# Small vectors in one load, a routing without POOL's splits, and a first weight chunk split under the last output tile

## The chip, the core and the metric

The kernel runs on one core of a Trainium2 chip. TensorE (PE, with its weight loads as PEld), VectorE (DVE), ScalarE (ACT), GpSimd (POOL) and SyncE (SP, which only issues loads here) work in parallel, each through its own list of instructions in a fixed order. The metric is the device time of one launch in microseconds; lower is better.

## The reference

One layer over 2048 tokens of width 1024: a modulated layer norm, a Hyena mixer (projection, short convolution, two long convolutions with filters that a small sine network makes, output projection), a residual with layer norm, and a mixture of 16 experts in which each expert chooses its 256 tokens. Cut to what the change touches:

```python
a = sin(freq * (z @ f_w1 + f_b1))                 # the filter network, three layers of 64
for n in range(2):
    a = sin(freq * (a @ f_w2[n] + f_b2[n]))
m = split(silu(c) @ mod_w + mod_b, 6)             # shift and scale of the layer norms
hl = layer_norm(x + pos) * (1 + m[1]) + m[0]
u = conv3(hl @ w_in + b_in, conv_w, conv_b)       # ... long convolutions, output projection, norm
aff = softmax(h @ w_router)                       # (2048, 16)
gate, idx = top_k(aff.T, 256)                     # expert choice: 256 tokens for each expert
xe = h[idx]
ye = ((silu(xe @ w1) * (xe @ w3)) @ w2) * gate    # w1, w3: 1024 x 2048, w2: 2048 x 1024, per expert
out = layer_norm(alpha * x + (1 + m[5]) * scatter_add(ye, idx))
```

All is fp32. A product of two fp32 matrices is made of three products of shortened numbers: `h` is the operand cast to fp32r, `l` what is left (operand minus cast), and hh + hl + lh is summed.

## The kernel before

The kernel is one long program for one core. Most of it goes through a scheduler that sets the order on each engine; the routing and the first expert's gathering stand in the order in which they are written (`manual_schedule`).

**Start (0 to about 117 us).** `early_mod` computes the shift and scale of the first norm: 16 loads `mw` of 512 KB (five buffers), of which five are multiplied with `sg` on PE (L462, 8 one-column products each) and eleven on DVE (`macc`, L464 and L467); 16 one-column products (L470) then sum `macc` over the partitions, and L473 adds `mb` and gives `md`. `filter_acts` runs the sine network in four pieces of 512 positions per layer: PE (L209), ACT `turn` (L211), two DVE steps `kk` (L213, L214), ACT sine (L215); its small vectors `fb` are six loads of four-byte elements on ACT's queue (L193 to L195). `side_steps` adds the position embedding to x on POOL (L496, L497), takes the statistics on DVE (L376, L377), makes 1/sqrt in `rstd_steps` (L383 to L392: `lva`, `lsq`, `r`, `nb`), normalises on ACT (L506), transposes on PE (L522) and modulates with `md` on ACT (L526). The projection's biases and convolution weights `prm` (L593 to L595) are loaded on ACT's queue too, and `cs` and `mb` (L445, L448) on SP's.

**Output stage (to about 1772 us).** 16 tiles of 128 tokens; of each tile two norms (`norm1`, `norm2`, L1167 to L1191), transposes (`turn`, L1221 and L1222), router logits (L1230, L1232) and their gathering (L1238, L1239). At n == 16 the generator `moe_start` loads the first expert's first chunk (SP) and makes POOL's constants and `tri`, `ii`, `blkb` (DVE, L1428 to L1430). After the loop, ACT loads the table for Exp (L1270).

**Routing (1772 to about 1847 us).** `phase_route` makes the softmax, packs each affinity into two 16-bit halves `half`, and searches the 256th largest of each expert two bits at a time: 7 rounds on the upper half, 8 on the lower. A round counts on DVE how many values reach each of three candidates (L1320, three instructions), sums the counts over an expert's partitions on PE (`cp`, L1322), compares with 256 (`ge` and `num`, L1338) and makes the next candidates (`base` L1335, `cand` L1342, with `thr` L1328 in the shadow of PE). Meanwhile the weights of chunks 0 and 1 of expert 0 are split: three casts each on ACT (L1400), three subtractions each on POOL (L1401).

**Experts (from about 1847 us).** Each of the 16 experts goes through 8 chunks of 256 hidden columns: SP loads w1, w3, w2 (L1391; two raw buffers for w1 and w3, one for w2), ACT casts and DVE subtracts, PE projects (L1502, L1503) and multiplies back (L175 to L177). `route(0)` comes first: it selects indices (PE, DVE), POOL gathers the 256 rows `xg` (L1472), PE transposes them in four groups through one PSUM buffer `tp` (L1482), and ACT and DVE split each group into `xs` (L1484, L1485).

## Time and profile before

| | us |
|---|---|
| median of 3 runs (lowest, highest) | 4089.68 (4086.54, 4090.18) |
| the profiled execution | 4085.04 |
| its span in the profile | 4083.2 |
| PE busy, whole span | 3833.0 (94%) |
| DVE busy | 2789.9 (68%) |
| ACT busy | 1940.8 (48%) |
| POOL busy | 1040.3 (25%) |
| start, 0 to 117: PE busy | 58.53 |
| middle, 117 to 1660: PE busy of 1543 | 1468.22 |
| output stage's end, 1660 to 1772: PE busy of 112 | 100.76 |
| routing and gathering, 1772 to 1847: PE busy of 75 | 8.03 |

The span runs from the first to the last instruction of the core; the profiled execution's own time has 1.84 us around it. PE is busy nearly all the time but for three places: the start, the routing, and the last 83 us. In those the other engines' order decides. Times in the rows below are microseconds from the start of the span.

### The profile page before, as it was taken

The page shows a single profiled execution, that of the slowest core. Times are in us where ns is not written, and L with a number is a line of the kernel's source. Part 1 is how long each engine was busy: PE and PEld are TensorE (multiplying, and loading weights), DVE is VectorE, ACT ScalarE, POOL GpSimd, SP SyncE. Part 2 cuts the span into 40 slices and gives each one's busy share as a digit, 9 for nine tenths or more (in the row PEclk, how much of TensorE's full clock was granted, in tenths as well). Part 3 has the DMA queues.
Part 4 walks back from the last instruction along what each step waited for, and adds up shares of the span by engine and source line. Part 5 has one row for each costly group of instructions (what it writes and reads, how often), then busy time and mean ns, then how long its engine had stood idle before and what let it go on. Part 6 is the DMA issues. An engine that isn't in the chain of part 4 may idle for free.

```text
span 4083.2 us, 52931 instructions
## 1 busy us (share of the span) xinstructions
PE 3833.0 (94%) x19839; PEld 3171.7 (78%) x19839; DVE 2789.9 (68%) x4017; ACT 1940.8 (48%) x2845; POOL 1040.3 (25%) x1092
## 2 busy tenths in 40 slices
PE   4899999999999989939999999999999999999997
PEld 3666766777777877827888888888888888888896
DVE  5777876776877877785666666666666666656766
ACT  3544543333777651114555555555555555544443
POOL 2355552212455442220000000000000000014635
PEclk8999999999999999969999999999999999999999
DMA  6355656667999986445666665666566656656764
GB/s 201 113 175 173 179 172 210 221 205 227 268 283 278 294 251 203 136 162 167 196 193 209 206 196 188 214 204 195 188 215 203 195 189 213 203 176 221 238 228 159
DMA packets 620796, 831.73 MB, mean 204 GB/s; under 512 B 56627, under 2 KB 506947, under 8 KB 618236
## 3 DMA queue, kind: packets, MB, share of 16 engines
q1 hardware_dynamic: 545594, 661.93, 50.8%
q0 software_dynamic: 57088, 163.48, 13.7%
q10 hardware_dynamic: 17858, 2.95, 0.5%
q8 instruction: 156, 2.56, 0.3%
q14 instruction: 100, 0.82, 0.1%
HBM read 643.82 MB, written 150.75 MB: 195 GB/s over the span
## 4 chain that ended last, share of the span: by engine, by line
PE 75%; DVE 9%; issue 5%; DMA 4%; POOL 3%; ACT 3%; SPq 0%; ACTq 0%; POOLq 0%; DVEq 0%
PE ab L1502 19%; PE ab L1503 10%; PE acc L175 5%; PE acc L176 5%; PE acc L177 5%; PE ip L175 3%; PE ip L177 3%; PE ip L176 3%; PE sp L335 2%; PE xp L854 2%; PE ap L889 2%; PE xp L872 2%; PE op L175 1%; PE op L177 1%; PE op L176 1%
## 5 line engine op out<-in xcount | busy, mean ns | idle before, releaser
L1502 PE MATMUL ab<-xs,w3h 128*128 128x512 f32 x1664 | 600.6, 399 | 0.0
L1502 PE MATMUL ab<-xs,w1h 128*128 128x512 f32 x1664 | 598.2, 399 | 0.0
L1401 DVE TENSOR_TENSOR w2l<-w2r,w2h 128x2048 fp32r<-128x2048 f32 x126 | 297.6, 2362 | 267.0 <-ACT w2h L1400 266.9
L1503 PE MATMUL ab<-xs,w3l 128*128 128x256 f32 x1664 | 468.2, 281 | 0.0
L1503 PE MATMUL ab<-xs,w1l 128*128 128x256 f32 x1664 | 466.6, 280 | 0.0
L175 PE MATMUL acc<-w2h,hh 128*128 128x512 f32 x1024 | 404.1, 395 | 14.3 <-ACT hh L170 13.8
L176 PE MATMUL acc<-w2l,hh 128*128 128x512 f32 x1024 | 402.5, 393 | 0.0
L177 PE MATMUL acc<-w2h,hl 128*128 128x512 f32 x1024 | 399.5, 391 | 0.8 <-DVE hl L171 0.8
L1502 PEld LDWEIGHTS ab<-xs,w3h 128*128 128x128 f32 x1664 | 313.0, 188 | 76.6
L1502 PEld LDWEIGHTS ab<-xs,w1h 128*128 128x128 f32 x1664 | 313.0, 188 | 72.9
L1548 POOL DMA_INDIRECT accd<-y,idx x27 | 68.5, 2535 | 1101.8 <-DVE y L1542 1095.6
L1401 DVE TENSOR_TENSOR w1l<-w1r,w1h 128x2048 fp32r<-128x2048 f32 x126 | 301.0, 2389 | 62.7 <-ACT w1h L1400 62.6
L170 ACT CAST hh<-u 128x256 fp32r<-128x256 f32 x256 | 104.1, 407 | 478.6 <-DVE u L1525 478.6
L1503 PEld LDWEIGHTS ab<-xs,w1l 128*128 128x128 f32 x1664 | 314.2, 189 | 7.1
L1506 DVE TENSOR_TENSOR u<-ab,u 128x256 f32<-128x256 f32 x416 | 174.6, 420 | 205.2 <-ACT u L1505 196.8
L1503 PEld LDWEIGHTS ab<-xs,w3l 128*128 128x128 f32 x1664 | 314.8, 189 | 0.0
L1401 DVE TENSOR_TENSOR w3l<-w3r,w3h 128x2048 fp32r<-128x2048 f32 x126 | 292.9, 2324 | 18.7 <-ACT w3h L1400 18.7
L1400 ACT CAST w2h<-w2r 128x2048 fp32r<-128x2048 f32 x128 | 244.1, 1907 | 94.7 <-PE acc L177 86.3
L1400 ACT CAST w1h<-w1r 128x2048 fp32r<-128x2048 f32 x128 | 244.5, 1910 | 80.5 <-PE ab L1502 79.0
L1400 ACT CAST w3h<-w3r 128x2048 fp32r<-128x2048 f32 x128 | 244.5, 1910 | 68.4 <-PE ab L1502 66.3
L1505 ACT COPY u<-ab 128x256 f32<-128x256 f32 x416 | 152.8, 367 | 184.9 <-PE ab L1503 184.8
L175 PE MATMUL ip<-hh,wh 128*128 128x512 f32 x576 | 237.4, 412 | 3.3 <-ACT hh L170 3.3
(399 smaller groups left out, 9114.7 us busy)
## 6 DMA issues: line engine op xcount, KB each, us to landing
w1r<-in_moe_w_dram SPq DMA_DIRECT2D x128, 1024.0 KB
w3r<-in_moe_w_dram SPq DMA_DIRECT2D x128, 1024.0 KB
w2r<-in_moe_w_dram SPq DMA_DIRECT2D x128, 1024.0 KB
fud<-ev SPq DMA_DIRECT2D x128, 256.0 KB
kr<-fud SPq DMA_DIRECT2D x64, 512.0 KB
bn<-ao POOLq DMA_DIRECT2D x248, 128.0 KB, 7.2
win<-in_c_win_dram SPq DMA_DIRECT2D x64, 256.0 KB
mw<-in_mod_w_dram SPq DMA_DIRECT2D x64, 256.0 KB
```

Source lines behind the costliest of these rows:

```text
L170: nc.scalar.copy(hi, raw)
L175: nc.tensor.matmul(out, lhsT=ah, rhs=bh, start=start, stop=False)
L176: nc.tensor.matmul(out, lhsT=ah, rhs=bl, start=False, stop=False)
L177: nc.tensor.matmul(out, lhsT=al, rhs=bh, start=False, stop=stop)
L335: nc.tensor.matmul(p, lhsT=s1[:, th], rhs=hb[th], start=True, stop=(n0 > 0))
L854: nc.tensor.matmul(p[:, i], lhsT=s2[:, 2 * gp + i], rhs=r[:, i], start=True, stop=True)
L1400: nc.scalar.copy(h, raw)
L1401: eng.tensor_tensor(l, raw, f_(h), OP.subtract)
L1502: nc.tensor.matmul(p, lhsT=ws[2 * j][:, k, fs], rhs=xs[:, k], start=(k == 0), stop=False)
L1503: nc.tensor.matmul(p[:, 0], lhsT=ws[2 * j + 1][:, k, fs], rhs=xs[:, k, 0], start=False, stop=(k == 7))
L1505: nc.scalar.copy(u, p[:, 1])
L1506: nc.vector.tensor_tensor(u, p[:, 0], u, OP.add)
```

## The change

1. **One load for small vectors.** The host lays c, mod_b, conv_w, conv_b, b_in, freq, b1 and b2 side by side in `c_small` (128 x 148), and SP loads it once in place of `cs`, `mb`, the six `fb` and the three `prm` loads.
2. **Small steps.** `kk` is one instruction of another kind (the scaled one with two tensors), and `rstd_steps` takes the square root with the constant as a bias on ACT, straight from `stat`, with fewer DVE steps behind it.
3. **End of the output stage.** Exp's table is loaded at n == 17, and there the casts of the first chunk's w1 and w3 (ACT) and their subtractions (DVE) are written; `tri`, `ii`, `blkb` follow them.
4. **Routing.** POOL's six subtractions are gone. The third count of a round is made on ACT (Sign with a sum), the other two on DVE count what lies below the candidate; PE sums them with two products; `ge` compares with a small tile `lim`; the third candidate's constants are 0.5 lower.
5. **Expert 0.** `route(0, wide=True)` puts groups 1 to 3 of the transposes into the three buffers `ab`; the cast of chunk 0's w2 stands on ACT behind the signs, its subtraction and those of chunk 1's w1 and w3 on DVE behind the splits of `xs`; chunk 1's w2 is split when chunk 1 is taken. On SP the load of chunk 2's w1 stands ahead of that of chunk 1's w2.

ACT's list at the start, before (the rows from the silu of c on; `fb`, `prm` are the small vectors, `fw`, `zt` the filter network's weights and input):

```order
L446 ACTIVATE sg<-cs 128x8
L193 DMA fb<-in_hy_f_freq_dram 64x1
L194 DMA fb<-in_hy_f_b_dram 64x1
L195 DMA fb<-in_hy_f_b_dram 64x2x1
...
L211 ACTIVATE turn<-sp,frq 128x512
L593 DMA prm<-in_hy_conv_w_dram 128x72x1
L594 DMA prm<-in_hy_conv_b_dram 128x24x1
L595 DMA prm<-in_hy_b_in_dram 128x24x1
L215 ACTIVATE a_459<-kk 128x512 x2
```

and now:

```order
L445 ACTIVATE sg<-small 128x8
L200 DMA zt<-in_c_z_dram 66x1024
L203 DMA fw_116<-in_hy_f_w_dram 64x64
L205 DMA fw_117<-in_hy_f_w_dram 64x64 x2
L203 DMA fw_116<-in_hy_f_w_dram 64x64
L205 DMA fw_118<-in_hy_f_w_dram 64x64 x2
L215 ACTIVATE turn<-sp,frq 128x512
L215 ACTIVATE turn<-g,frq 128x512
L215 ACTIVATE turn<-sp,frq 128x512
L219 ACTIVATE a_446<-kk 128x512
```

Nine issues of small loads have left ACT's list, three of them from between the first turns and the first sine.

PE's list at the start, before, from the fourth `mw` product's neighbours to the transposes of x (`a` and `zt` hold the first and second layer's results):

```order
L209 MATMUL sp<-a_459,fw_119 128x512
L209 MATMUL g<-a_459,fw_119 128x512
L462 MATMUL sd<-sg,mw 128x1 x8
L209 MATMUL sp<-a_459,fw_119 128x512
L209 MATMUL g<-a_459,fw_119 128x512
L470 MATMUL sd<-ones_f,macc_170 128x1 x8
L470 MATMUL sd<-ones_f,macc_171 128x1 x8
L209 MATMUL sp<-zt,fw_120 128x512
L209 MATMUL sp<-zt,fw_121 128x512
L522 MATMUL sd<-ident,x 128x128 x16
```

and now, the same stretch:

```order
L459 MATMUL sd<-sg,mw 128x1 x8
L213 MATMUL sp<-zt,fw_117 128x512
L213 MATMUL sp<-zt,fw_118 128x512
L213 MATMUL g<-zt,fw_117 128x512
L213 MATMUL g<-zt,fw_118 128x512
L213 MATMUL sp<-zt,fw_117 128x512
L213 MATMUL sp<-zt,fw_118 128x512
L467 MATMUL sd<-ones_f,macc_163 128x1 x8
L467 MATMUL sd<-ones_f,macc_164 128x1 x8
L519 MATMUL sd<-ident,x 128x128 x32
```

Six products of the network's third layer now stand ahead of the sums over the partitions, where before two stood behind them.

ACT's list at the end of the output stage, before (`ht` and `lp`, `lg` belong to the last tile's transposes and logits):

```order
L1179 ACTIVATE r<-r 128x1
L1239 COPY lg<-rp 128x32
L1222 COPY ht<-tp 128x4x128 x2
L1232 COPY lp<-rp 128x256
L1239 COPY lg<-rp 128x32
L1270 ACT_TABLE_LOAD
L1270 ACTIVATE r<-ident 128x1
L1287 ACTIVATE lg<-lg 128x256
L1400 CAST w1h<-w1r 128x2048
L1400 CAST w3h<-w3r 128x2048
L1400 CAST w2h<-w2r 128x2048
```

and now:

```order
L1175 ACTIVATE r<-r 128x1
L1256 ACT_TABLE_LOAD
L1256 ACTIVATE r<-ident 128x1
L1437 CAST w1h<-w1r 128x2048
L1437 CAST w3h<-w3r 128x2048
L1235 COPY lg<-rp 128x32
L1218 COPY ht<-tp 128x4x128 x2
L1228 COPY lp<-rp 128x256
L1235 COPY lg<-rp 128x32
L1285 ACTIVATE lg<-lg 128x256
L1318 ACTIVATE sign,cs<-half_15054,kc 128x256
L1318 ACTIVATE sign,cs<-half_15054,cand 128x256 x6
```

The table load and two casts have moved ahead of the last tile's copies, and signs stand where the casts of both chunks stood.

The diff, cut to its core:

```diff
@@ -166,6 +166,16 @@
+def host_small(x):
...
+    col = lambda v: np.asarray(v, dtype=np.float32).reshape(-1, 128).T
+    two = lambda v: np.concatenate([np.asarray(v, dtype=np.float32).reshape(-1, 64).T] * 2, 0)
+    return np.ascontiguousarray(np.concatenate(
+        [col(x["c"][0]), col(x["mod_b"][0, 0:2048]), col(x["hy_conv_w"][0]), col(x["hy_conv_b"][0]), col(x["hy_b_in"][0]),
+         two(x["hy_f_freq"][0]), two(x["hy_f_b1"][0]), two(x["hy_f_b2"][0])], 1))
@@ -177,10 +187,9 @@
+def filter_acts(tc, A, fb, ld, ps, afw, arv):
-    fb = ld.tile([128, 4], F32, name="fb")
@@ -188,11 +197,6 @@
-    for s in range(2):
-        sl = slice(s * 64, s * 64 + 64)
-        nc.scalar.dma_start(fb[sl, 0:1], A["hy_f_freq"][0].unsqueeze(1))
-        nc.scalar.dma_start(fb[sl, 1:2], A["hy_f_b1"][0].unsqueeze(1))
-        nc.scalar.dma_start(fb[sl, 2:4], A["hy_f_b2"][0].rearrange("i k -> k i"))
@@ -211,7 +215,7 @@
-        nc.vector.tensor_tensor(kk, turn, kk, OP.subtract)
+        nc.vector.scalar_tensor_tensor(kk, kk, -1.0, turn, op0=OP.mult, op1=OP.add)
@@ -379,16 +383,13 @@
-    va = wk.tile([128, n], F32, name="lva")
-    nc.vector.tensor_scalar(va, stat[:, :, 1], eps, None, op0=OP.add)
+    nc.scalar.activation(r, stat[:, :, 1], AF.Sqrt, bias=eps)
+    yield 1
...
-    nc.scalar.activation(sq, va, AF.Sqrt)
-    yield 1
-    nc.vector.reciprocal(r, sq)
-    nc.vector.tensor_tensor(sq, r, r, OP.mult)
-    nc.vector.tensor_tensor(sq, sq, va, OP.mult)
-    nc.vector.tensor_scalar(sq, sq, -0.5, 1.5, op0=OP.mult, op1=OP.add)
-    nc.vector.tensor_tensor(r, r, sq, OP.mult)
+    nc.vector.reciprocal(r, r)
+    nc.vector.scalar_tensor_tensor(sq, stat[:, :, 1], eps, r, op0=OP.add, op1=OP.mult)
+    nc.vector.scalar_tensor_tensor(sq, sq, -0.5, r, op0=OP.mult, op1=OP.mult)
+    nc.vector.scalar_tensor_tensor(r, sq, 1.5, r, op0=OP.add, op1=OP.mult)
@@ -589,10 +588,7 @@
-        prm = S.top.tile([128, 5, 24], F32, name="prm")
-        nc.scalar.dma_start(prm[:, 0:3], A["hy_conv_w"][0].rearrange("j (k p) -> p j k", p=128))
-        nc.scalar.dma_start(prm[:, 3], A["hy_conv_b"][0].rearrange("(k p) -> p k", p=128))
-        nc.scalar.dma_start(prm[:, 4], A["hy_b_in"][0].rearrange("(k p) -> p k", p=128))
+        prm = S.small[:, 24:144].rearrange("p (j k) -> p j k", j=5)
@@ -1256,7 +1252,8 @@
-            if n == 16:
+            if n == 17:
+                nc.scalar.activation(wk.tile([128, 1], F32, name="r"), ident[:, 0:1], AF.Exp)
@@ -1266,8 +1263,6 @@
-        sq = wk.tile([128, 1], F32, name="r")
-        nc.scalar.activation(sq, ident[:, 0:1], AF.Exp)
@@ -1281,11 +1276,13 @@
+        lim = wk.tile([128, 3], F32, name="lim")
+        nc.gpsimd.memset(lim[:, 0:2], T - CAP + 0.5)
+        nc.gpsimd.memset(lim[:, 2:3], T - 2.0 * CAP + 1.0)
...
-        next(R.split_first)
@@ -1314,12 +1311,17 @@
-                cnt = wk.tile([128, 3], BF16, name="cnt", bufs=2)
-                for k in range(3):
+                cnt = wk.tile([128, 2], BF16, name="cnt", bufs=2)
+                cs = wk.tile([128, 1], BF16, name="cs", bufs=2)
+                sign = wk.tile([128, 256], BF16, name="sign")
+                with nc.allow_low_precision(reason="whole numbers of at most 256"):
+                    nc.scalar.activation(sign, v, AF.Sign, scale=-1.0, bias=cand[:, 2:3], accum_out=cs)
+                for k in range(2):
...
-                    nc.vector.tensor_scalar(junk, v, cand[:, k:k + 1], 0.0, op0=OP.is_ge, op1=OP.add, accum_out=cnt[:, k:k + 1])
+                    nc.vector.tensor_scalar(junk, v, cand[:, k:k + 1], 0.0, op0=OP.is_lt, op1=OP.add, accum_out=cnt[:, k:k + 1])
...
-                nc.tensor.matmul(p, lhsT=blkb, rhs=cnt, start=True, stop=True)
+                nc.tensor.matmul(p[:, 2:3], lhsT=blkb, rhs=cs, start=True, stop=True)
+                nc.tensor.matmul(p[:, 0:2], lhsT=blkb, rhs=cnt, start=True, stop=True)
@@ -1335,7 +1337,7 @@
-                nc.vector.tensor_scalar(ge, p, CAP - 0.5, 0.0, op0=OP.is_ge, op1=OP.add, accum_out=num)
+                nc.vector.scalar_tensor_tensor(ge, p, 1.0, lim, op0=OP.mult, op1=OP.is_le, accum_out=num)
@@ -1422,18 +1424,30 @@
-            nc.gpsimd.memset(R.kc[:, n, k:k + 1], float((k + 1) << (14 - 2 * n)))
+            nc.gpsimd.memset(R.kc[:, n, k:k + 1], float((k + 1) << (14 - 2 * n)) - 0.5 * (k == 2))
...
+    hs = [(n, raw, wt.tile(list(raw.shape), F32R, name=n + "h"), wt.tile(list(raw.shape), F32R, name=n + "l")) for n, raw in raws]
...
+    def sub(i):
+        _, raw, h, l = hs[i]
+        nc.vector.scalar_tensor_tensor(l, raw, 1.0, f_(h), op0=OP.mult, op1=OP.subtract)
...
+    for i in range(2):
+        nc.scalar.copy(hs[i][2], hs[i][1])
+    for i in range(2):
+        sub(i)
...
+    R.first = [t for h in hs for t in h[2:]]
...
-    R.first = []
-    for n in range(2):
-        R.first.append(split(raws, nc.gpsimd))
-        if n == 0:
-            raws = load(0, 1)
+    nc.scalar.copy(hs[2][2], hs[2][1])
+    yield
+    sub(2)
+    raws = load(0, 1)
+    R.second = split(raws[:2])
+    R.raw = raws[2:]
@@ -1441,14 +1455,15 @@
-        with tc.manual_schedule():
-            phase_route(tc, ident, ones_f, lg, R)
+        order = st.enter_context(ExitStack())
+        order.enter_context(tc.manual_schedule())
+        phase_route(tc, ident, ones_f, lg, R)
@@ -1475,7 +1490,7 @@
-                p = ps.tile([128, 2, 256], F32, name="tp", bufs=1)
+                p = ps.tile([128, 2, 256], F32, name="ab", bufs=3) if wide and q else ps.tile([128, 2, 256], F32, name="tp", bufs=1)
@@ -1586,9 +1601,14 @@
-        with tc.manual_schedule():
-            for _ in route(0):
-                pass
+        first = route(0, wide=True)
+        next(first)
+        next(R.split_first)
+        next(first)
+        for _ in first:
+            pass
+        next(R.split_first)
+        order.close()
@@ -1603,7 +1623,10 @@
-                ws = R.first.pop(0) if R.first else R.split(R.load(e, fc))
+                if e == 0 and fc < 2:
+                    ws = (R.second + R.split(R.raw)) if fc else R.first
+                else:
+                    ws = R.split(R.load(e, fc))
@@ -1740,6 +1763,8 @@
+            S.small = S.top.tile([128, 148], F32, name="small")
+            nc.sync.dma_start(S.small, A["c_small"])
```

## Rows read from the trace of the kernel before

**Rows 1.** Windows: us, busy of PE, PEld, DVE, ACT, POOL, clock, DMA, GB/s

```profile
1772.00:1847.00 75.00, 8.03 (x35) 5.60 (x36) 60.01 (x206) 13.47 (x11) 28.96 (x8) 0.51 0.50 168
1847.00:4000.00 2153.00, 2139.80 (x11961) 1853.33 (x11961) 1365.86 (x1665) 1079.22 (x1364) 267.66 (x226) 1.00 0.63 202
```

**Rows 2.** Timeline, ACT, start: start, us, instruction, idle before, releaser

```profile
24.28 0.78 ACT L211 ACTIVATE turn<-sp,frq 128x512 f32<-128x512 f32 x1 [19.03 <-DMA fw<-in_hy_f_w_dram]
...
25.60 15.20 ACTq L594 DMA_DIRECT2D prm<-in_hy_conv_b_dram  x1
...
43.01 1.15 ACT L215 ACTIVATE a<-kk 128x512 f32<-128x512 f32 x2 [16.61 <-issue]
```

**Rows 3.** Timeline, PE, start of the kernel

```profile
12.41 3.55 PE L462 MATMUL sd<-sg,mw 128*128 128x1 f32 x16 [10.54 <-DMA mw<-in_mod_w_dram]
15.81 2.06 PE L209 MATMUL sp<-zt,fw 66*128 66x512 f32 x2
...
47.07 1.84 PE L462 MATMUL sd<-sg,mw 128*128 128x1 f32 x16
...
56.78 6.99 PE L470 MATMUL sd<-ones_f,macc 128*128 128x1 f32 x32 [6.04 <-DVE macc L467]
77.30 3.78 PE L209 MATMUL sp<-zt,fw 128*128 128x512 f32 x4 [13.53 <-ACT zt L215]
```

**Rows 4.** Timeline, DVE, start of the kernel

```profile
63.80 0.24 DVE L473 SCALAR_TENSOR_TENSOR md<-sd,mb 128x8 f32<-128x8 f32 x2 [4.62 <-PE sd L470]
...
67.02 8.04 DVE L383 TENSOR_SCALAR lva<-stat 128x4 f32<-128x4 f32 x1
...
80.31 0.15 DVE L392 SCALAR_TENSOR_TENSOR nb<-stat,r 128x4 f32<-128x4 f32 x1
```

**Rows 5.** Timeline, POOL, start: the first of six such additions in a row

```profile
67.69 1.27 POOL L496 TENSOR_TENSOR x<-x,pr 128x512 f32<-128x512 f32 x1
```

**Rows 6.** Timeline, ACT, end of the output stage and start of the routing

```profile
1767.94 0.58 ACT L1222 COPY ht<-tp 128x512 f32<-128x512 f32 x1 [4.07 <-PE tp L1221]
...
1772.03 1.28 ACT L1270 ACT_TABLE_LOAD   x1
...
1773.43 0.40 ACT L1287 ACTIVATE lg<-lg 128x256 f32<-128x256 f32 x1
1773.74 1.88 ACT L1400 CAST w1h<-w1r 128x2048 fp32r<-128x2048 f32 x1
```

**Rows 7.** Timeline, DVE, last output tile, first routing step, first expert

```profile
1760.82 0.22 DVE L1428 TENSOR_SCALAR tri<-ii 128x128 f32<-128x128 int32 x1
...
1772.05 0.42 DVE L1285 TENSOR_REDUCE mx<-lg 128x16 f32<-128x256 f32 x1 [5.37 <-ACT lg L1239]
...
1859.44 2.29 DVE L1401 TENSOR_TENSOR w1l<-w1r,w1h 128x2048 fp32r<-128x2048 f32 x1 [1.55 <-ACT w1h L1400]
```

**Rows 8.** Timeline, POOL, routing: first two of six subtractions in a row

```profile
1775.71 4.52 POOL L1401 TENSOR_TENSOR w1l<-w1r,w1h 128x2048 fp32r<-128x2048 f32 x1 [43.18 <-ACT w1h L1400]
1780.17 4.52 POOL L1401 TENSOR_TENSOR w3l<-w3r,w3h 128x2048 fp32r<-128x2048 f32 x1
```

**Rows 9.** Timeline, DVE, rounds of the routing

```profile
1776.28 0.48 DVE L1320 TENSOR_SCALAR_CACHE_REDUCE junk<-half,kc 128x256 uint16<-128x256 uint16 x1
...
1780.35 4.35 DVE L1342 SCALAR_TENSOR_TENSOR cand<-num,base 128x3 f32<-128x3 f32 x1
...
1803.39 0.48 DVE L1320 TENSOR_SCALAR_CACHE_REDUCE junk<-half,cand 128x256 uint16<-128x256 uint16 x1
...
1803.80 0.47 DVE L1320 TENSOR_SCALAR_CACHE_REDUCE junk<-half,cand 128x256 uint16<-128x256 uint16 x1
...
1805.34 0.48 DVE L1320 TENSOR_SCALAR_CACHE_REDUCE junk<-half,cand 128x256 uint16<-128x256 uint16 x1
```

**Rows 10.** Timeline, PE, start of expert 0

```profile
1843.66 0.90 PE L1482 MATMUL tp<-ident,xg 128*128 128x128 f32 x3 [1.74 <-DMA xg<-xnd,idx]
...
1860.19 0.40 PE L175 MATMUL acc<-w2h,hh 128*128 128x512 f32 x1
```

More of the change, by code (lines that the diff above doesn't have):

```diff
@@ L177, in mm3 @@
     nc.tensor.matmul(out, lhsT=al, rhs=bh, start=False, stop=stop)
-def filter_acts(tc, A, ld, ps, afw, arv):
+def filter_acts(tc, A, fb, ld, ps, afw, arv):
     nc = tc.nc
-    fb = ld.tile([128, 4], F32, name="fb")
     zt = ld.tile([128, T], F32, name="zt")[0:66]
@@ L439, in late_mod, with early_mod @@
         yield
-def early_mod(nc, A, md, sg, ones_f, wk, ps):
-    cs = wk.tile([128, 8], F32, name="cs", bufs=1)
-    nc.sync.dma_start(cs, A["c"][0].rearrange("(k p) -> p k", p=128))
+def early_mod(nc, A, cs, mb, md, sg, ones_f, wk, ps):
     nc.scalar.activation(sg, cs, AF.Silu)
-    mb = wk.tile([128, 2, 8], F32, name="mb", bufs=1)
-    nc.sync.dma_start(mb, A["mod_b"][0, 0:2048].rearrange("(i k p) -> p i k", i=2, p=128))
     yield
@@ L503, in norm @@
         nb = wk.tile([128, 4], F32, name="nb")
-        yield from rstd_steps(nc, wk, r, nb, stat, ADALN_EPS, 4)
+        yield from rstd_steps(nc, wk, r, nb, stat, eps, 4)
         for j in range(4):
@@ L537, in side_steps @@
         pr = wk.tile([128, 512], F32, name="pr", bufs=1)
+        eps = wk.tile([128, 1], F32, name="eps", bufs=1)
+        nc.vector.memset(eps, ADALN_EPS)
         nc.gpsimd.dma_start(pr, A["c_posr"])
@@ L1449, in phase_moe, with route @@
         ps = st.enter_context(tc.tile_pool(reuse_waits="tile", name="e_ps", bufs=2, space=PSUM))
-        def route(e):
+        def route(e, wide=False):
             oh = wk.tile([128, 256], F32, name="oh", bufs=1)
@@ L1753, in build @@
                         tc.tile_pool(reuse_waits="tile", name="m_wk", bufs=2, side="right") as mk:
-                    mod = early_mod(nc, A, md, sg, ones_f, mk, sps)
+                    mod = early_mod(nc, A, S.small[:, 0:8], S.small[:, 8:24].rearrange("p (i k) -> p i k", i=2), md, sg, ones_f, mk, sps)
                     next(mod)
-                    acts = filter_acts(tc, A, ld, fps, afw, arv)
+                    acts = filter_acts(tc, A, S.small[:, 144:148], ld, fps, afw, arv)
                     side = side_steps(tc, A, md, ident, S, psum, h2d)
@@ L1800 @@
     given.update(host_consts())
+    given["c_small"] = host_small(given)
+    for n in ("c", "hy_conv_w", "hy_conv_b", "hy_b_in", "hy_f_freq", "hy_f_b1", "hy_f_b2"):
+        del given[n]
     for n, a in given.items():
```

## The prediction

> **What bounds the kernel now.** I read the busy times by stage first, then the timelines of each engine in the stages where PE stands still. Between 1847 and 4000 us PE is busy 2139.80 of 2153 us [rows 1]: nothing of this change can gain there, it can only lose. Between 1772 and 1847 us PE is busy 8.03 of 75 us [rows 1]; there the chain runs through the routing's rounds on DVE. The start is the other such stage: PE ends its sums over the partitions at 56.78 + 6.99 = 63.77 us, `md` follows at 63.80, `nb`, with which ACT can normalise the first x, only at 80.31 [rows 3, 4]. So the change is worth what it takes from two chains, the start's up to `nb` and the routing's. Where a stage's end moves by a microsecond, everything behind it moves along, as PE has no slack later.
>
> **The start (vectors in one load, `kk`, `rstd_steps`).** The load of conv_b alone occupies ACT's queue from 25.60 for 15.20 us, and the first sine comes at 43.01 after 16.61 us of idle ACT [rows 2]. These 16.6 us do not all return, because PE itself is late next. By the new list it has to do, ahead of the sums L467: five `mw` products at 3.40 (12.41 to 15.81) and eight products of the first two layers at 2.06 [rows 3], together 17.0 + 16.5 = 33.5 us; then six products of the third layer, which at 77.30 took 3.78 / 2 = 1.89 each and at the higher speed at which an `mw` product took 1.84 instead of 3.40 would take 1.02 [rows 3]: 6.1 to 11.3 us, taken as 8; then the sums, 6.99 as they were or, by the same ratio, 3.8, taken as 5.3. PE's first product waits until 12.41 for the first `mw`, which stands on SP behind the thousands of four-byte elements of c and mod_b; these go. I let PE start at 6.5, an estimate, about half of the present 12.4, which stays as the other end. So `md` comes at 6.5 + 33.5 + 8 + 5.3 = 53.3 instead of 63.8: -10.5.
>
> From `md` to `nb` it is 16.5 us now. In it DVE's `lva`, a 128 x 4 instruction, lasts 8.04 us [rows 4]: from 67.69 on POOL does six additions of 1.27 without a gap [rows 5], and `lva` ends as the last of them does. `lva` itself is gone, but the new `lsq` and `r` steps read two tensors and stand in the same place. In the new list the load that starts POOL's burst (`wraw`, which waits for DVE's `wl`) has four additions behind it instead of six, 5.1 us; I take the stretch as 11 us: -5.5. Last, two sines (1.15 / 2 = 0.58 each [rows 2]) and two `turn` steps (about as long) now stand ahead of the normalising on an ACT that then works without a break: -2.0 to -2.4. Together -18. Bounds: if PE starts at 12.4 and keeps the low speed, `md` comes at 12.4 + 33.5 + 11.3 + 7.0 = 64.2, nothing is won there, and -8 is left; if all of ACT's idle time, the shorter burst and the 2.4 come back, -25.
>
> **POOL's hold on the routing.** The first round begins at 1776.28, the fourth at 1803.39 [rows 9]: 27.1 us for three rounds. A round without POOL takes 1805.34 - 1803.39 = 1.95 us [rows 9]. The trace shows whose the difference is: `cand`, three numbers wide, takes 4.35 us and ends at 1784.70; POOL's second subtraction ends at 1780.17 + 4.52 = 1784.69 [rows 8, 9]. At the pace of these, 1780.17 - 1775.71 = 4.46, the sixth ends at 1802.5, just before the fourth round. The count at 1776.28 ran inside the first subtraction and took only 0.48, so POOL holds some DVE instructions, not all [rows 8, 9]. POOL's six subtractions go, and what is left on it there are two small fills. Three rounds at 1.95 and the two extra instructions in them (a copy and a fill, at 0.48 at most) make 6.8: -20.3, with bounds of -19 and -21.
>
> **The third count on ACT.** DVE's counts follow each other by 1803.80 - 1803.39 = 0.41 [rows 9], and a round loses one: 15 x 0.40 = -6.0. ACT has no such count in the trace; a pass of 128 x 256 took it 0.40 [rows 6], and reading the sum comes on top. It has the 0.41 + 0.47 = 0.88 us that two DVE counts last; the product of its count stands ahead of theirs on PE. The hold begins above 0.88, and at 1.3 us (three DVE counts) nothing is won. The bounds are -6 and, with a second product of at most 0.16 in each round uncovered, +2.4. I take -6, since 0.40 is far from 0.88.
>
> **Around the last output tile.** Exp's table leaves the path: the Exp at 1773.43 can follow DVE's two steps, the first of which takes 0.42 from 1772.05 on and the second as long, at 1772.9 [rows 6, 7]: -0.5. What moves into the last tile costs ACT 1773.43 - 1772.03 = 1.40 for table and first Exp and 2 x 1.88 for casts, 5.2 us, and ACT was idle for 4.07 there [rows 6]: 1.1 too much. But `tri` at 1760.82 and its two successors (0.22 each) stood ahead of the last tile's norm on DVE and now stand behind it: 0.65 earlier. Net +0.4, between -0.65 and +1.4. DVE's two subtractions, 2.29 each, fit with the three small ones into its 5.37 us of idle time [rows 7].
>
> The trace's table load takes 1.28 us, and the next ACT instruction ends it with no further wait [rows 6]. The Trainium skill ("ScalarE: Activation LUTs", What ACT_TABLE_LOAD costs) says that a switch costs about 2.7 us with its drain. By the page the last tile's copies would be 1.4 us later still, and the total 4045.9; the trace disagrees, and I go by it.
>
> **Expert 0.** The transposes no longer wait for one buffer: from the landing of the second gather, 1843.66, it took 16.5 us to the first product of w2 at 1860.19 [rows 10], and four groups with four buffers save at most a round trip or two: -0.8. Against it stand three more subtractions on DVE, 3 x 2.29 = 6.9 us [rows 7], ahead of the first gating product; they are hidden as long as they end within the first chunk's projection, which fills most of those 16.5 us. If that cover fails, I put 2.5 us, one subtraction. Bounds -2 and +2.5.
>
> **Sum.** -18 - 20.3 - 6.0 - 0.5 + 0.4 - 0.8 = -45.2. The profiled execution took 4085.04, so 4039.8. The median of the runs, 4089.68, lies 4.64 above that execution; the changed kernel's median is then 4044.5. By the lower bounds of the parts it is about 4033, by the upper ones about 4067.
>
> **Rivals.** *The start gives its gain back* (17%). The loads of `mw` remain 8 MB through five buffers, and PE remains at low speed with products that are mostly weight loads. For it: PE waited 10.54 us for the first `mw` [rows 3], and six more products stand ahead of the sums. Against it: the chain was interrupted for 16.6 us by ACT's queue alone. With -8 instead of -18 the time is 4054.5, with worse luck at expert 0 4060.
>
> *The count on ACT gains nothing* (10%): handing `cand` to ACT and its count to PE uses up the 0.88 us. For it: two more hand-overs between engines in each round. Against it: 0.40 for a pass. 4050.5, or 4053 with the second product uncovered.
>
> *The start gives more* (10%): PE reaches its higher speed early, and `md` comes before 50. 4029 to 4036.
>
> *The table switch as the page has it* (4%): 4046.
>
> *The long DVE steps were not POOL's* (3%), but a wait for PE or a semaphore that stays: 4064. The ends that coincide to 0.02 us speak against it.
>
> *Slower* (4%): the split weights fall behind at expert 0, since chunk 1's splits no longer happen during the routing, and never catch up. Every one of the 128 chunks would then wait; from 0.35 us per chunk on (45.2 / 128) the gain is gone, and at 0.5 us it is 64 - 45 = 19 us slower, about 4108. Against it: with 13 us of idle in 2153 [rows 1], PE has found its weights ready chunk after chunk with the same lists and buffers, so a lead that is lost once is found again.
>
> **How the numbers follow.** The forecast, 4044.5 with its own range of 4036 to 4052, has 52%. The range of 8 in 10 reaches to the start's two other cases, 4030 to 4065. A measurement of this kernel can tell about 0.2% (8 us) from no change: faster by more than that 94%, within it 2%, slower 4%.
>
> **What would show it.** In the new profile: the first sine before 25 us, `md` near 53 and `nb` near 64; no routing instruction on DVE over 0.5 us, 15 rounds of about 1.55; the sum of the count on ACT ready before DVE's second; the routing stage 27 us shorter; PE's first product of w2 16 us behind the second gather. If `md` stays above 60, the first term is wrong; if rounds stay at 1.95, the third is; if PE shows more idle time after expert 0 than before, the slower case has come.

## The result and the profile after

The changed kernel took 4045.39 us (median of 4 runs, 4042.53 to 4048.78) against 4089.93 (4086.54 to 4093.45) for the kernel before: a ratio of 0.9891, 95% interval 0.9874 to 0.9908. Forecast were 4044.5 within 4030 to 4065. In the profile the span is 4040.8 us after 4083.2, 42.4 shorter.

How far the changed kernel is ahead of the one before can be read at the same piece of work in both traces: 21.2 us at POOL's load of `wraw` behind the first tiles (119.21 and 98.06), 14.5 at the end of POOL's constants for the routing (1732.52 and 1717.99), 39.8 at the first gather of expert 0 (1836.77 and 1796.94), 41.1 where that expert's results are added (1991.12 and 1950.00), 41.1 to 42.6 from there to the end. So the time went out of the two places that the prediction named, and 6.6 us came back between them, which it did not name.

The start first, PE's timeline; it answers to [rows 3]:

```profile
7.09 3.55 PE L459 MATMUL sd<-sg,mw 128*128 128x1 f32 x16 [5.21 <-DMA mw<-in_mod_w_dram]
...
41.96 1.88 PE L213 MATMUL sp<-zt,fw 128*128 128x512 f32 x4
43.68 3.63 PE L467 MATMUL sd<-ones_f,macc 128*128 128x1 f32 x32
```

PE begins at 7.09 instead of 12.41, and the sums begin at 43.68 instead of 56.78. They take 3.63 us instead of 6.99. DVE's timeline, which answers to [rows 4]:

```profile
47.34 0.24 DVE L470 SCALAR_TENSOR_TENSOR md<-sd,small 128x8 f32<-128x8 f32 x2 [2.27 <-PE sd L467]
...
52.78 5.54 DVE L390 SCALAR_TENSOR_TENSOR lsq<-stat,eps,r 128x4 f32<-128x4 f32 x1
...
59.99 0.15 DVE L393 SCALAR_TENSOR_TENSOR nb<-stat,r 128x4 f32<-128x4 f32 x1
```

`md` is 16.5 us earlier than before, `nb` 20.3. What stands between them now is `lsq`, a step of four columns, with 5.54 us. POOL's timeline at that time (compare [rows 5]):

```profile
52.42 0.94 POOL L568 DMA_DIRECT2D wraw<-in_hy_w_in_dram  x1 [1.38 <-DVE r L389]
53.38 1.27 POOL L493 TENSOR_TENSOR x<-x,pr 128x512 f32<-128x512 f32 x1
...
57.04 1.25 POOL L494 TENSOR_TENSOR x<-x,pc 128x512 f32<-128x512 f32 x1
```

Four additions follow the load instead of six, and `lsq` ends at 58.32, with the last of them (57.04 + 1.25).

The routing, DVE's timeline; it answers to [rows 9]:

```profile
1762.50 0.48 DVE L1321 TENSOR_SCALAR_CACHE_REDUCE junk<-half,kc 128x256 uint16<-128x256 uint16 x1
...
1763.97 0.16 DVE L1344 SCALAR_TENSOR_TENSOR cand<-num,base 128x3 f32<-128x3 f32 x1
1764.17 0.48 DVE L1321 TENSOR_SCALAR_CACHE_REDUCE junk<-half,cand 128x256 uint16<-128x256 uint16 x1
...
1765.71 0.48 DVE L1321 TENSOR_SCALAR_CACHE_REDUCE junk<-half,cand 128x256 uint16<-128x256 uint16 x1
...
1767.61 0.48 DVE L1321 TENSOR_SCALAR_CACHE_REDUCE junk<-half,cand 128x256 uint16<-128x256 uint16 x1
...
1783.12 0.48 DVE L1321 TENSOR_SCALAR_CACHE_REDUCE junk<-half,cand 128x256 uint16<-128x256 uint16 x1
...
1784.27 0.16 DVE L1340 SCALAR_TENSOR_TENSOR ge<-cp,lim 128x3 f32<-128x3 f32 x1
...
1784.54 0.16 DVE L1344 SCALAR_TENSOR_TENSOR cand<-num,base 128x3 f32<-128x3 f32 x1
1784.74 0.48 DVE L1321 TENSOR_SCALAR_CACHE_REDUCE junk<-half,cand 128x256 uint16<-128x256 uint16 x1
```

The first three rounds take 1767.61 - 1762.50 = 5.1 us instead of 27.1. `cand` lasts 0.16. The first rounds are 1.54 apart (1764.17 to 1765.71), the later ones 1.62 (1783.12 to 1784.74). ACT's part in the same stretch and at the end of the output stage ([rows 6] are its rows before):

```profile
1749.19 1.28 ACT L1256 ACT_TABLE_LOAD   x1
...
1750.59 1.88 ACT L1437 CAST w1h<-w1r 128x2048 fp32r<-128x2048 f32 x1
1752.38 1.89 ACT L1437 CAST w3h<-w3r 128x2048 fp32r<-128x2048 f32 x1
...
1754.26 1.07 ACT L1218 COPY ht<-tp 128x512 f32<-128x512 f32 x2
...
1759.64 0.42 ACT L1285 ACTIVATE lg<-lg 128x256 f32<-128x256 f32 x1 [1.01 <-DVE lg L1284]
...
1784.82 0.51 ACT L1318 ACTIVATE sign<-half,cand 128x256 bf16<-128x256 uint16 x1 [1.01 <-DVE cand L1344]
1785.23 0.19 ACT L1318 ACTIVATION_READ_ACCUMULATOR sign<-half,cand 128x1 bf16 x1
```

A count on ACT takes 0.51 and the reading of its sum 0.19: 1784.82 to 1785.42, and DVE's second count ends with its reading at 1785.63. ACT is ready first. Table and casts fill ACT from 1749.19 to 1754.27, and only then come the last tile's copies.

### The profile page after: what moved, and what is told of

It reads as the page before. It is cut to its first block, busy times and chain, and to the rows that moved or that the text cites. A ratio compares the mean times of both kernels' runs of the same rounds, so it can differ in the third digit from the quotient of the medians.

```text
span 4040.8 us, 52974 instructions
## 1 busy us (share of the span) xinstructions
PE 3839.0 (95%) x19854; PEld 3175.7 (79%) x19854; DVE 2780.5 (69%) x3986; ACT 1951.0 (48%) x2875; POOL 1015.1 (25%) x1088
## 3 DMA queue, kind: packets, MB, share of 16 engines
q0 software_dynamic: 57088, 163.48, 13.8%
## 4 chain that ended last, share of the span: by engine, by line
PE 75%; DVE 7%; issue 5%; DMA 4%; POOL 4%; ACT 3%; SPq 0%; POOLq 0%; ACTq 0%; DVEq 0%
PE ab L1517 19%; PE ab L1518 10%; PE acc L185 5%; PE acc L186 5%; PE acc L187 5%; PE ip L185 3%; PE ip L187 3%; PE ip L186 3%; PE sp L339 2%; PE xp L850 2%; PE xp L868 1%; PE ap L885 1%; PE op L185 1%; PE op L187 1%; PE op L186 1%
## 5 line engine op out<-in xcount | busy, mean ns | idle before, releaser
L1403 DVE TENSOR_TENSOR w3l<-w3r,w3h 128x2048 fp32r<-128x2048 f32 x127 | 295.2, 2324 | 18.7 <-ACT w3h L1402 18.7
```

The costliest lines, as they stand in the source:

```text
L1403: eng.tensor_tensor(l, raw, f_(h), OP.subtract)
```

## Experiments

**Which part gives what.** Four kernels each hold a part of the change. `start_only` is the kernel before with parts 1 and 2, `old_start` the changed kernel without them, `loads_only` and `steps_only` are parts 1 and 2 alone. Their diffs are pieces of the one for the whole change, taken over whole: the loads (`host_small`, `filter_acts`, `early_mod`, `prm`), or `kk` and `rstd_steps` with `eps`. `prm_only` takes only `prm` from the one load:

```diff
-        nc.scalar.dma_start(prm[:, 0:3], A["hy_conv_w"][0].rearrange("j (k p) -> p j k", p=128))
-        nc.scalar.dma_start(prm[:, 3], A["hy_conv_b"][0].rearrange("(k p) -> p k", p=128))
-        nc.scalar.dma_start(prm[:, 4], A["hy_b_in"][0].rearrange("(k p) -> p k", p=128))
+        prm = S.small[:, 24:144].rearrange("p (j k) -> p j k", j=5)
```

> The kernel before with parts 1 and 2 of the change alone (one load for the small vectors, the new kk and rstd_steps). Theory: the start is worth what the changed kernel's trace shows there, nb near 60 us instead of 80.3 and the load of the convolution's first constants about 21 us earlier, and of these 21 some 6 to 7 are lost again in the middle stage because every engine there meets later stores and loads at another moment: 4075, give or take 3. Rival: what the middle stage lost was the chance of one execution, and the start keeps its 21: 4069. Rival: the start's gain needs part 3 to 5 and is under 10 us alone: 4080 or more.

> The changed kernel with parts 1 and 2 undone: the old loads, kk and rstd_steps, with the new end of the output stage, routing and expert 0. Theory: the start is as before (nb near 80), the routing's rounds are as in the changed kernel, and the time is 4090 - 27 = 4063 (26 in the routing, 1 at expert 0), with the middle stage as long as before. Rival, if the middle stage's loss comes with parts 3 to 5 in some way: 4069.

> The kernel before, where prm alone (conv_w, conv_b, b_in) comes out of the one load of small vectors; cs, mb and the six fb are loaded as before, and kk and rstd_steps are as before. Theory: the three prm loads on ACT's queue hold the first sine back by 16.6 us, but PE, which starts its products at 12.4 because cs and mb stand ahead of mw, and the sums over the partitions are late next; md comes at 56 to 60 instead of 63.8 and the start is 4 to 8 us shorter: 4082 to 4086. Rival: prm was the whole matter, md comes before 50 and the start is 15 or more us shorter: 4075 or less.

> The kernel before with part 1 alone: all small vectors come out of one load; kk and rstd_steps as before. The two parts together made the start 18.6 us shorter in the trace (to POOL's wraw load at 119 us), and the middle stage behind it 6.7 us longer (1599.7 against 1593.0). Theory: the loads are the start's gain (16 of 18.6, md near 50), the steps give the rest; and if the longer middle stage comes with any start in which the order of the first tiles moves, it is here too, about 1599: 4076. Rival: the longer middle stage comes from the steps (rstd_steps is used for the later tiles too), and stays at 1590 to 1593 here: 4070.

> The kernel before with part 2 alone: the new kk and rstd_steps, the loads as before. Theory: the start is 2 to 4 us shorter (two additions less behind the wraw load, so the hold on DVE is 5.5 instead of 8.0 us), and the middle stage is as before, 1593: 4084 to 4086. Rival: the middle stage is 6 to 7 us longer with these steps: 4090 or more.

Measured, with the kernel before at 4087.52 in the runs of the first three and at 4088.94 in those of the last two; "ahead" is how far each is in front of the first profile of before at the `wraw` load (119.21), "middle stage" the time from there to a point 20.1 us ahead of POOL's last constant for the routing (that constant starts at 1732.29 in that profile, which makes 1593.0):

| | median, us | ratio (95%) | ahead at the start's end | middle stage |
|---|---|---|---|---|
| start_only | 4072.34 | 0.9960 (0.9949 to 0.9971) | 18.6 | 1599.7 |
| old_start | 4059.15 | 0.9935 (0.9918 to 0.9951) | 1.2 | 1591.8 |
| prm_only | 4081.09 | 0.9987 (0.9977 to 0.9997) | 6.8 | 1589.7 |
| loads_only | 4075.13 | 0.9968 (0.9955 to 0.9980) | 18.4 | 1597.3 |
| steps_only | 4087.43 | 0.9996 (0.9986 to 1.0006) | 3.3 | 1599.1 |

The two halves add up: 15.2 us from the start, 28.4 from the rest, 43.6 together, where the whole change gave 44.5. The start's gain is the loads'; the steps alone cannot be told from no change. The shorter burst on POOL is the loads' too: in `loads_only` four additions follow the `wraw` load and hold a step for 4.94 us, while in `steps_only` six still follow it, against the expectation, and the held step, there a `kk`, lasts about as long as `lva` did. DVE in `steps_only`:

```profile
65.95 7.97 DVE L214 SCALAR_TENSOR_TENSOR kk<-kk,turn 128x512 f32<-128x512 f32 x1
```

And the gain of the loads is not `prm` alone, though `prm` alone held the first sine back most: without it the sine comes at 27.71 instead of 43.01, but PE gets its first `mw` at 14.78. PE in `prm_only`:

```profile
14.78 3.54 PE L472 MATMUL sd<-sg,mw 128*128 128x1 f32 x16 [5.45 <-DMA mw<-in_mod_w_dram]
...
50.25 6.99 PE L480 MATMUL sd<-ones_f,macc 128*128 128x1 f32 x32 [6.71 <-DVE macc L477]
```

What this kernel still loads in four-byte elements costs the rest: c and mod_b ahead of `mw` on SP, and the six `fb` loads on ACT's queue, behind which the first `turn` comes at 24.46 instead of 15.58. In the changed kernel, without both, `mw` is there at 7.09. No run separates the two.

**Why the sums take 3.6 or 7.0 us.** In `start_only`, PE's products end earlier than in the changed kernel, and the sums still end later:

```profile
37.32 1.88 PE L213 MATMUL sp<-zt,fw 128*128 128x512 f32 x4
43.20 6.99 PE L467 MATMUL sd<-ones_f,macc 128*128 128x1 f32 x32 [4.01 <-DVE macc L464]
```

PE stood still for 4.01 us until DVE's last `macc`, and the sums took 6.99 us. The windows of the sums in both (us, PE, PEld, DVE, ACT, POOL busy with counts, granted clock, DMA, GB/s), the changed kernel first:

```profile
43.70:47.30 3.60, 3.60 (x33) 3.52 (x31) 1.38 (x3) 2.33 (x2) 1.19 (x1) 1.00 1.02 395
```

```profile
43.20:50.20 7.00, 6.99 (x32) 6.90 (x32) 1.82 (x3) 2.33 (x2) 4.48 (x4) 0.50 1.04 399
```

With the granted clock at 1.00 (2.4 GHz) they take half the time that they take at 0.50 (1.2 GHz). In all fourteen traces it is the same: where products ran up to the sums without a pause (the changed kernel twice, `loads_only`, `adds_on_dve`, `both`, `pool_reads`, `pool_fills`) they took 3.63, where PE had waited 3 to 7 us just before (before twice, `start_only`, `old_start`, `prm_only`, `steps_only`, `count_on_dve`) they took 6.99. The same kernel start fell on either side, since it is a matter of whether PE's products or DVE's `macc` are late by a few microseconds.

**The third count.** The count goes back to DVE, in the new form:

```diff
-        nc.gpsimd.memset(lim[:, 2:3], T - 2.0 * CAP + 1.0)
+        nc.gpsimd.memset(lim[:, 2:3], T - CAP + 0.5)
...
-                cnt = wk.tile([128, 2], BF16, name="cnt", bufs=2)
...
-                    nc.scalar.activation(sign, v, AF.Sign, scale=-1.0, bias=cand[:, 2:3], accum_out=cs)
-                for k in range(2):
+                cnt = wk.tile([128, 3], BF16, name="cnt", bufs=2)
+                for k in range(3):
...
-                nc.tensor.matmul(p[:, 2:3], lhsT=blkb, rhs=cs, start=True, stop=True)
-                nc.tensor.matmul(p[:, 0:2], lhsT=blkb, rhs=cnt, start=True, stop=True)
+                nc.tensor.matmul(p, lhsT=blkb, rhs=cnt, start=True, stop=True)
```

> The changed kernel with the third count on DVE again (is_lt, like the other two) and one product for all three sums; the rest as changed, POOL's splits gone. Theory: each round is 1.95 us as in the undisturbed rounds before, against 1.62 in the changed kernel: 15 x 0.33 = 5.0 us more in the routing, 4050. Rival: the count on ACT gains nothing, because ACT has its results only when DVE would have them: 4045.

4051.08 us (4049.56 to 4052.14), ratio 0.9911 (0.9894 to 0.9927): 5.7 more than the changed kernel's 4045.39. The medians alone leave the size open, as the two ran beside different runs of before (36.4 us ahead of it here, 44.5 there). In the traces, between POOL's last constant and the first gather, it gains 20.0 us on before, the changed kernel 25.3. The count on ACT is worth 5.3 there, near the 15 x 0.33 = 5.0 of the expectation.

**Is it POOL that holds DVE, and what on POOL?** Both kernels put work of POOL beside the first rounds of the changed kernel's routing, on a scratch tile whose contents nobody uses:

```diff
+        dm = wk.tile([128, 2048], F32, name="dm")
+        nc.gpsimd.memset(dm, 0.0)
+        nc.gpsimd.tensor_copy(dm[:, 0:256], lgf)
+        for _ in range(6):
+            nc.gpsimd.tensor_tensor(dm, dm, dm, OP.subtract)
```

and with twelve times `nc.gpsimd.memset(dm, 0.0)` in place of the subtractions.

> The changed kernel with six subtractions 128 x 2048 on POOL beside the routing's first rounds, on a scratch tile that nobody else reads; no cast and no weight is involved. Theory: POOL's subtractions themselves hold DVE: base, cand and thr take 2 to 4.5 us each while they last, the counts 0.48, and the routing's first rounds are about 20 us longer: 4065. Rival: what held DVE before were the weights' data or ACT's casts beside them, and rounds stay at 1.62: 4045.

> The changed kernel with twelve fills (memset) of the same scratch tile on POOL in that place, which read nothing. Theory: what holds DVE is POOL's reading two operands, and with fills no routing instruction on DVE is longer than 0.5 us: 4045. Rival: any long instruction on POOL holds them, writing alone too, and the first rounds are longer by as much as the fills last (20 us or so): 4065.

With subtractions 4060.58 us, with fills 4048.81 (one run each). DVE and POOL beside the subtractions:

```profile
1762.63 21.99 POOL L1303 TENSOR_TENSOR dm<-dm 128x2048 f32<-128x2048 f32 x6
```

```profile
1764.21 2.05 DVE L1342 TENSOR_SCALAR base<-kc,thr 128x3 f32<-128x3 f32 x1
...
1766.36 3.57 DVE L1349 SCALAR_TENSOR_TENSOR cand<-num,base 128x3 f32<-128x3 f32 x1
...
1770.77 2.84 DVE L1335 SCALAR_TENSOR_TENSOR thr<-num,thr 128x1 f32<-128x1 f32 x1
...
1773.64 3.65 DVE L1342 TENSOR_SCALAR base<-kc,thr 128x3 f32<-128x3 f32 x1
...
1786.56 0.23 DVE L1342 TENSOR_SCALAR base<-kc,thr 128x3 f32<-128x3 f32 x1
```

and beside the fills:

```profile
1764.48 22.32 POOL L1303 MEMSET dm<- 128x2048 f32 x12
```

```profile
1766.41 0.16 DVE L1349 SCALAR_TENSOR_TENSOR cand<-num,base 128x3 f32<-128x3 f32 x1
...
1769.26 0.16 DVE L1335 SCALAR_TENSOR_TENSOR thr<-num,thr 128x1 f32<-128x1 f32 x1
...
1771.39 0.53 DVE L1342 TENSOR_SCALAR base<-kc,thr 128x3 f32<-128x3 f32 x1
...
1777.92 1.50 DVE L1312 TENSOR_SCALAR above<-half,thr 128x256 uint16<-128x256 uint16 x1
```

While the six subtractions run (22.0 us), `base`, `cand` and `thr` last 2.0 to 3.7 us each, as in [rows 9]; the subtractions touch no weight, and no cast runs beside them. With fills for 22.3 us `cand` and `thr` last 0.16. Steps with one tensor operand are longer: `base` takes 0.53 instead of 0.23, `above` 1.50 instead of 0.28. Both end with a fill, within 0.06 us: at 1.86 us each the fourth ends at 1771.92, the eighth at 1779.36. So the hold was POOL's, and for the two-operand steps it takes POOL's subtraction, which reads; a long POOL instruction that reads a single operand was not tried. The Trainium skill has this as a rule ("SBUF — State Buffer", SBUF: two separate sides): a DVE instruction in a two-port mode, or one with two SBUF operands against a GpSimd instruction that reads SBUF, and the GpSimd instruction exclude each other for the whole length of an instruction. Both runs agree with it on the two-operand steps; that `base` and `above` run in a two-port mode no row shows. In the routing a held step ends with the subtraction that runs. At the start one step was held over four additions in a row (5.54 us) or six (8.04); why, no run shows.

**Taking the hold out of the start.** The last two tiles of the second quarter get their position embedding on DVE:

```diff
-            nc.gpsimd.tensor_tensor(x[:, 0:512], x[:, 0:512], pr, OP.add)
-            nc.gpsimd.tensor_tensor(x[:, 512:1024], x[:, 512:1024], pc, OP.add)
+            eng = nc.vector if quarter == 1 and j > 1 else nc.gpsimd
+            eng.tensor_tensor(x[:, 0:512], x[:, 0:512], pr, OP.add)
+            eng.tensor_tensor(x[:, 512:1024], x[:, 512:1024], pc, OP.add)
```

> The changed kernel, where the position embedding of the second quarter's last two tiles is added on DVE (four additions of 0.69) and not on POOL. Theory: POOL has then nothing behind its wraw load that holds DVE, lsq takes 0.2 us instead of 5.5, and nb follows md by 8 us instead of 12.6, although DVE has two of the four additions ahead of nb: 4041. Rival: DVE's own additions and what they push back eat it up, nb follows md by 11 or more: 4045.

4040.05 us (4037.24 to 4045.20), ratio 0.9887 (0.9871 to 0.9904); the changed kernel, again on the same chip, 4042.15. DVE:

```profile
47.58 0.24 DVE L470 SCALAR_TENSOR_TENSOR md<-sd,small 128x8 f32<-128x8 f32 x2 [2.30 <-PE sd L467]
...
53.02 0.20 DVE L390 SCALAR_TENSOR_TENSOR lsq<-stat,eps,r 128x4 f32<-128x4 f32 x1
...
53.80 0.68 DVE L494 TENSOR_TENSOR x<-x,pr 128x512 f32<-128x512 f32 x1
...
55.15 0.15 DVE L393 SCALAR_TENSOR_TENSOR nb<-stat,r 128x4 f32<-128x4 f32 x1
```

`lsq` takes 0.20, and `nb` follows `md` by 7.6 us instead of 12.65; at the end of the start the kernel is 27.3 us ahead of before. The 5 us are plain in the trace; the medians (2.1 apart) cannot separate the two kernels.

DVE steps are longer beside POOL at an earlier place too, which this kernel leaves alone. The new start brings the `kk` steps forward to where POOL adds the first tiles' embedding (17.51 to 27.08). DVE in the changed kernel, the last line without POOL beside it:

```profile
18.31 2.90 DVE L217 TENSOR_SCALAR kk<-turn 128x512 f32<-128x512 f32 x2
21.12 3.43 DVE L218 SCALAR_TENSOR_TENSOR kk<-kk,turn 128x512 f32<-128x512 f32 x2
...
32.44 1.28 DVE L218 SCALAR_TENSOR_TENSOR kk<-kk,turn 128x512 f32<-128x512 f32 x2
```

In the changed kernel the profile lists no wait of PE from 7.09 to 47.31. In `start_only`, where PE waited 4.01 us for DVE, the same two steps take 2.90 and 3.43; whether they made that wait was not tested.

**And a lighter last tile.** `both` adds to this that of the last tile's two casts only that of w1 stays there. The cast of w3 goes behind the Exp, and its subtraction into the wait for the gathered rows:

```diff
...
-    for i in range(2):
-        nc.scalar.copy(hs[i][2], hs[i][1])
-    for i in range(2):
-        sub(i)
+    nc.scalar.copy(hs[0][2], hs[0][1])
+    sub(0)
...
+    nc.scalar.copy(hs[1][2], hs[1][1])
+    yield
     nc.scalar.copy(hs[2][2], hs[2][1])
     yield
+    sub(1)
     sub(2)
     raws = load(0, 1)
-    R.second = split(raws[:2])
+    R.second = split(raws[:1])
+    yield
+    R.second += split(raws[1:2])
...
```

> adds_on_dve, and in the last output tile only the cast and subtraction of w1: the cast of w3 stands behind the Exp on ACT, its subtraction and those of chunk 0's w2 and chunk 1's w1 on DVE in the wait for the gathered rows. Theory: the last tile's copies no longer wait for ACT (5.1 us of inserted work becomes 3.3), which gives 1.2 us ahead of the routing, and two subtractions less stand ahead of the first gating product at expert 0: 4039 to 4040. Rival: the cast of w3 pushes the first sign back, or the subtractions in the gather's wait (6.9 us in 7.4) push back the splits of xs, and the routing stage is as long as in the changed kernel: 4041.

4043.03 us (4042.01 to 4044.21), ratio 0.9890 (0.9874 to 0.9907). The last tile's copies wait for PE's transposes again (0.19 us), not for ACT, and the routing begins 1.8 us earlier, measured from the end of the middle stage. It is lost again: at PE's first product with w1 (1807.01, in the changed kernel 1807.51), measured from the same point, it is 1.0 us behind. The subtractions in the gather's wait free buffers for weights, and SP loads into them at once. SP, PE and POOL:

```profile
1796.60 0.37 SPq L1395 DMA_DIRECT2D w3r<-in_moe_w_dram  x1
1798.76 0.37 SPq L1395 DMA_DIRECT2D w2r<-in_moe_w_dram  x1
```

```profile
1798.05 0.45 PE L1502 MATMUL tp<-ident,xg 128*128 128x128 f32 x1 [5.38 <-DMA xg<-xnd,idx]
1803.05 0.90 PE L1502 MATMUL tp<-ident,xg 128*128 128x128 f32 x3 [4.55 <-DMA xg<-xnd,idx]
```

```profile
1795.06 2.32 POOL L1492 DMA_INDIRECT xg<-xnd,idx  x1 [0.30 <-issue]
```

and POOL in the changed kernel:

```profile
1798.42 0.97 POOL L1487 DMA_INDIRECT xg<-xnd,idx  x1 [0.30 <-issue]
```

The second gather's rows come 5.0 us behind the first's (1803.05 and 1798.05), in the changed kernel 2.0 (1803.54 and 1801.52), where SP issued no load from 1765 to 1810. Of these 3.0 us, 1.35 are POOL's second gather instruction itself, 2.32 instead of 0.97; beside it DVE makes the subtraction of w3 (1794.24 to 1796.52), which the changed kernel does not have there. That the rest is the loads' is likely but not tested.

**Is the middle stage's length the kernel's own?** Both kernels once more, without an edit:

> The changed kernel once more, for the spread of one kernel's profiled executions. In seven kernels with the new start the middle stage (from POOL's wraw load behind the first tiles to the last such point before the routing) was 1597 to 1600 us, in before's profile 1593.0. Theory: the length of the middle stage belongs to the kernel; here it is 1599.6 within 1, and the time is 4045. Rival: it is chance from one execution to the next, and here it lies anywhere from 1590 to 1600. In the trace of the changed kernel the sums over the partitions took 3.63 us where other kernels with the same start took 6.99; if that is chance too, md comes at 50 instead of 47.3.

> The kernel before once more, for the same question. Theory: its middle stage is 1593.0 within 1. Rival: it is chance, and here it is 1595 or more, as the median of its runs, 4 us above the first profiled execution, would let expect.

The changed kernel took 4042.15 us (4036.84 to 4046.36), ratio 0.9889 (0.9872 to 0.9905), the kernel before 4086.32 in the same rounds and 4082.39 in its profiled run. The middle stage was 1594.4 us in the changed kernel's second trace and 1599.6 in its first; 1592.0 and 1593.0 in those of before. So two executions of one kernel differ by 5 us there, against the expectation, and the 6.6 us that the first pair of traces shows as given back are not a measure of the change. In the first trace 3.0 of the 6.6 are lost at one step, where ACT stands idle for 3.62 us until stores of `ht` (`h2d`) have landed; in the first trace of before that wait was 0.64:

```profile
201.84 1.02 ACT L523 ACTIVATE ht<-g,md 128x256 f32<-128x256 f32 x2 [3.62 <-DMA h2d<-ht]
```

```profile
219.32 1.02 ACT L526 ACTIVATE ht<-g,md 128x256 f32<-128x256 f32 x2 [0.64 <-DMA h2d<-ht]
```

The second trace of the changed kernel has this wait too (3.45 us at 204.00), so the 5 us by which its two traces differ lie elsewhere.

With the new start the stage was 1594 to 1602 us in nine traces, with the old one or a part of it 1590 to 1599 in five. The medians point to a part that stays: `start_only` and `loads_only` gain 15.2 and 13.8 us where their traces are 18.6 and 18.4 ahead at the start's end. How much of it comes with the new start stays open.

## Why the prediction was right

*The start, -18.* In six traces with the changed start it was 18.3 (`pool_reads`, `pool_fills`), 18.6 (`start_only`), 18.7 (`count_on_dve`), 18.8 (changed kernel, second time) and 21.2 (first time), each against the first trace of before; against the second, which reached that point 1.3 us earlier, it is 1.3 less. The size is right, its parts less so. PE started at 7.1 (6.5 forecast). Its products took 36.6 us up to the sums, not 41.5, since part of them ran at the higher clock; the sums took 3.6 or 7.0 where 5.3 was taken for both. `md` came at 47.3 or at 50.2 to 50.5 instead of 53.3. That PE and DVE's last `macc` would be late together was not seen: the forecast took PE alone. From `md` to `nb` it was 12.3 to 12.75 instead of 11; the hold of the four additions was there with 5.5 us, 5.1 forecast. The rival "the start gives more" had the right mechanism, a higher clock early, and in the first trace 3 of the 8 us that it gave itself. "The start gives its gain back" did not come about.

*POOL's hold, -20.3.* The first three rounds lost 22.0 us, of which 1.2 is the third count: 20.8. `pool_reads` brings the long steps back, `pool_fills` does not.

*The third count, -6.0.* 5.3. The rounds are 0.33 shorter, not 0.40: from the third round on `cand` starts 0.27 behind `ge` (1784.27 and 1784.54), in the first rounds 0.20. Probably `cand`, whose tile has two buffers, now waits for ACT's reading of the older one too; that was not tested. ACT is not the limit, against the rival that gave it 10%.

*Exp and the last tile, -0.5 and +0.4.* The Exp's part was right: from DVE's first routing step to the Exp it takes 0.97 us (1758.67 to 1759.64) instead of 1.38, since the wait for the table load is gone. The last tile came out worse: the step that failed is that 0.65 us of earlier norm would nearly pay for 1.1 us of ACT. The norm's first steps did come earlier on DVE, but its square root `r` stands on ACT behind the copies `ht` of the tile before, and starts 31.2 us after POOL's last constant in both traces (1763.51 and 1748.96). So the 0.65 never reached the path, and between `r` and the routing's first instruction 1.2 us were lost, about the 1.1 without it. `both`, with one cast there instead of two, gets 1.8 us back.

*Expert 0, -0.8.* 1.3 between the first gather and the adding of the expert's results. The sign the prediction gave for it was wrong: PE's first product of w2 came 19.3 us behind the second gather, not 16; the new list has more of the next projection ahead of it, and PE had no idle time in between.

*The sum* was -45.2, and the medians say -44.5 and -44.2. It came out so well because the large terms were read apart in the profile. Part of it is luck: in the first pair of profiles the start gained 3 us more than forecast and the middle stage gave back 6.6, which the forecast had at nothing, and the spans differ by 42.4; the medians lie closer to the forecast than these. *Slower* did not come about: from expert 0's results on, the lead stays between 41.1 and 42.6 us. Two sums of the prediction do not come out as stated: its bounds add up to 4034.5 and 4068.5, not 4033 and 4067, and 4060 for the first rival needs 5.5 us at expert 0, where its own bound allows 3.3.

## What to carry to other kernels

A short DVE instruction that takes microseconds beside a POOL instruction that reads is a hold; the ends coincide to hundredths, and moving a few additions from POOL to DVE can be cheaper than leaving them "off the critical path" (5 us in the trace here). Loads of four-byte elements can cost twice: on the engine whose queue issues them (15.20 us on ACT's for conv_b), and, as far as these runs show, for whatever stands behind them on the same queue. Work that is put into a wait frees its inputs' buffers, and the loads that this starts, like the work itself, run beside whatever the wait was for.

## What the runs showed of the hardware

A 128 x 256 Sign with a sum took ACT 0.51 us and the reading of its sum 0.19. On POOL, six subtractions 128 x 2048 with one operand for both inputs took 22.0 us (3.7 each), where those of two tiles took 4.5; a fill of that tile took 1.86. A POOL fill does not hold two-operand DVE steps, but holds some with one operand: 1.50 us for `above`, which takes 0.28. The sums over the partitions took 3.63 us at a granted clock of 1.00 and 6.99 at 0.50.
